# Strassen's seven products for the down projection of a hybrid decoder layer

## The chip, the cores and the metric

The kernel runs on one core of a Trainium2 chip. The metric is device time in microseconds (us) for one execution of the whole layer; a smaller time is better. The engines are named as in the profile: PE (TensorE, with PEld for its weight loads), DVE (VectorE), ACT (ScalarE), POOL (GpSimd) and SP (SyncE, which here only issues transfers).

## What is computed

The layer takes x (512 tokens by 1024 features, float32), adds the output of two mixers (an mLSTM group and a sparse-attention group), and then a gated MLP, on which the change works:

```python
h = rms_norm(x, norm_ffn[l])
u = causal_dwconv(h @ w_up[l], ffn_conv_w[l], ffn_conv_b[l])   # 1024 -> 2 * 2816, conv of width 3
gate, val = u[..., :D_FF], u[..., D_FF:]
x = x + (jax.nn.silu(gate) * val) @ w_down[l]                  # 2816 -> 1024
...
return rms_norm(x, norm_final)
```

## The kernel before

Every float32 product is made as three products of rounded parts: each operand is split into a high part (ACT copies it to the fp32r type: `whi`, `gh`) and a low part (DVE or POOL subtracts the high part from it: `wlo`, `gl`), and PE adds high·high, low·high and high·low into one PSUM bank. `split` (L121) makes the two parts.

Weights come from DRAM in pieces of 1 MB (`raw`, two buffers, issued by SP), and each piece is split in two halves of 128x1024, into four buffers of `whi` and four of `wlo`. All engines follow one order that is written out in the code, each engine its own part of it in sequence, so an instruction that waits holds up all behind it on its engine. `take` hands out the next split piece and puts splits of pieces up to two ahead into a queue, `later`; `merge` pops one entry of it after each step of PE's work.

The up projection has 44 groups (22 chunks of 128 features, a gate and a value for each). A group is 24 matmuls of 512 columns into one of three banks (tags mm, mm, av). Behind each group ACT and DVE do the convolution from the bank (`conv3`, L999); for a gate ACT also does the silu; for a value POOL multiplies gate and value (L1018), and the product is split into `gh` and `gl` (22 chunks x 512 tokens).

The down projection holds eight accumulators, 4 tiles of 128 tokens x 2 halves of 512 features, in all eight banks. It runs over 22 chunks; a chunk needs one split weight piece and makes 8 x 3 = 24 matmuls of 512 columns (L1053 to L1055). The last four chunks are done tile by tile, so that the final norm of a tile (square on ACT, mean, gain, power on POOL, scale, store) lies beside the matmuls of the next; the last 512 columns are done as two pieces of 256.

Of the kernel before, what the change touches and what calls it, by code (L numbers as in the profile page):

```python
# [44 lines left out]
def hybrid_layer(ctx: ExitStack, tc: tile.TileContext, a, out):  # L45
# [14 lines left out]
    def bank(tag):  # L60
        return ps.tile([128, 512], F32, name="bank_" + tag, tag=tag, bufs={"mm": 2, "lg": 3, "tp": 2, "av": 1}[tag])
# [5 lines left out]
        return bank(mm_tags[-1])  # L67


    raws, subs, nload, nsplit = [], [], [0], [0]  # L70

    def add_raw(pieces, cuts, place=None):

        raws.append([pieces, place])
        for view, shape in cuts:
            subs.append([len(raws) - 1, view, shape, None])

    def load_to(n):
        while nload[0] < min(n, len(raws)):
            i = nload[0]  # L80
            raw = raws[i][1]
            if raw is None:
# [21 lines left out]
    def split_next():  # L104
        i = nsplit[0]
        r, view, shape, _ = subs[i]
        load_to(r + 1)
        src = view(raws[r][1])
        cnt = shape[0] * shape[1]
        hi = wp.tile([128, 1024], F32R, name="whi", tag="whi", bufs=4)  # L110
        lo = wp.tile([128, 1024], F32R, name="wlo", tag="wlo", bufs=4)
        hv = hi[:, :cnt].rearrange("p (a b) -> p a b", a=shape[0])
        lv = lo[:, :cnt].rearrange("p (a b) -> p a b", a=shape[0])

        split(hv, lv, src, nc.gpsimd if i in on_pool else None)
        subs[i][3] = (hv, lv)
        nsplit[0] += 1
        if i + 1 < len(subs) and subs[i + 1][0] != r:
            load_to(r + 3)
# [58 lines left out]
    for c2 in range(NF // 2):  # L178
        add_raw(rows(a["w_down"], 2 * c2), [row_cut(0), row_cut(1)])
    sub_i, look = [0], [2]  # L180
    on_pool = set(range(6, 25)) | {35,37,39}

# [822 lines left out]
    ys = {}  # L1005
# [40 lines left out]
    banks = [bank(tag) for tag in ("lg", "lg", "lg", "tp", "tp", "av", "mm", "mm")]  # L1046
    gh, gl = ffn["gh"], ffn["gl"]

    def down(c, t, hf, w, b_=None, c0=0, c1=512, first=0):
        sl, cs = slice(t * 128, (t + 1) * 128), slice(c0, c1)  # L1050
        wh, wl = w
        b_ = (b_ or banks[2 * t + hf])[:, cs]
        nc.tensor.matmul(b_, gh[:, c, sl], wh[:, hf, cs], start=(c == first), stop=False)  # L1053
        nc.tensor.matmul(b_, gl[:, c, sl], wh[:, hf, cs], start=False, stop=False)  # L1054
        nc.tensor.matmul(b_, gh[:, c, sl], wl[:, hf, cs], start=False, stop=(c == NF - 1))  # L1055

    for c in range(NF - 4):
        (w,) = take()
        for t in range(NB):
            for hf in range(2):  # L1060
                down(c, t, hf, w)
            if later:
                later.popleft()()
    o_v = out.rearrange("b (t p) d -> (b t) p d", p=128)
    ws = take(4)
    for t in range(NB):
        pieces = ((0, 0, 512), (1, 0, 512)) if t < NB - 1 else ((0, 0, 512), (1, 0, 256), (1, 256, 512))
        ssf = small.tile([128, 3], F32, name="ssf")
        xn = ffn["p"].tile([128, D], F32, name="xn", tag="yc", bufs=3)
        for i, (hf, c0, c1) in enumerate(pieces):  # L1070

            own = bank("lg") if c0 else None
            for j in range(4):
                down(NF - 4 + j, t, hf, ws[j], own, c0, c1, NF - 4 if c0 else 0)
            cs = slice(hf * 512 + c0, hf * 512 + (c1 if c0 else 512))
            nc.vector.tensor_tensor(x[t][:, cs], (own or banks[2 * t + hf])[:, c0:(c1 if c0 else 512)], x[t][:, cs], OP.add)
            cs = slice(hf * 512 + c0, hf * 512 + c1)
            nc.scalar.activation(xn[:, cs], x[t][:, cs], AF.Square, accum_out=ssf[:, i:i + 1])

            ms = small.tile([128, 1], F32, name="ms", bufs=4)  # L1080
            if i == 0:
                nc.vector.tensor_scalar(ms, ssf[:, 0:1], 1.0 / D, EPS, op0=OP.mult, op1=OP.add)
            else:
                nc.vector.scalar_tensor_tensor(ms, ssf[:, i:i + 1], 1.0 / D, last, op0=OP.mult, op1=OP.add)
            last = ms
            (nc.vector if i + 1 == len(pieces) else nc.gpsimd).tensor_tensor(x[t][:, cs], x[t][:, cs], gfin[hf][:, c0:c1], OP.mult)
        r = small.tile([128, 1], F32, name="r", bufs=4)
        nc.gpsimd.tensor_tensor(r, last, mhalf[:, :1], OP.pow)
# [36 lines left out]
```

## Time and profile before

| | |
|---|---|
| time, median of 3 runs (lowest, highest) | 673.66 us (672.49, 675.17) |
| the profiled execution | 673.75 us, its span 672.0 us |
| busy share of the span: PE, DVE, ACT, POOL | 97 %, 60 %, 44 %, 23 % |
| bytes moved by transfers | 62.22 MB, 93 GB/s on average |

A page of the profile gives the busy time of each engine, and a chain of work followed back from the last instruction. Busy time of PE is modelled for each matmul with its start and length, and matmuls overlap; what counts is the distance between starts. An idle time is shown in brackets behind the instruction that ended it, with what released it.

### The profile page before, as it was taken

Reading aid. Unit: us, or ns where it says so; the run is one execution under the profiler, and the core shown is the slowest. Engines: PE = TensorE matmul, PEld = TensorE weight load, DVE = VectorE, ACT = ScalarE, POOL = GpSimd, SP = SyncE. Lnnn points to the kernel's source line nnn. Section 1 sums busy time; section 2 is a strip of 40 time slices with the busy share of each in tenths; the row PEclk is TensorE's granted clock in tenths of the full one; section 3 lists DMA queues with packets and bytes.
Section 4 is the critical chain, followed back from the end, with each engine's and each line's share of the span. In section 5 each row is a group of like instructions: output and inputs, shape, how many; then the busy total and the mean of one; then the engine's idle time right before and its main releaser. Section 6 shows DMA issues by size and latency. Waiting matters only on the chain.

```text
span 672.0 us, 8948 instructions
## 1 busy us (share of the span) xinstructions
PE 654.9 (97%) x3455; PEld 559.4 (83%) x3455; DVE 403.2 (60%) x741; ACT 296.3 (44%) x510; POOL 157.0 (23%) x162
## 2 busy tenths in 40 slices
PE   7999999989999999999999999999999999999996
PEld 5987889768889998889888888888888888888885
DVE  4688999979756765765465555555555562222234
ACT  5555255756756424453444453444444441111223
POOL 2132576223452306322101101010101110000023
PEclk9999999989999999999999999999999999999998
DMA  9321543010111221313033312331133233322102
GB/s 300 124 66 62 176 139 123 3 64 1 63 63 54 74 81 46 90 68 126 1 125 126 110 58 83 126 126 62 63 126 125 91 130 134 117 88 101 62 32 94
DMA packets 47194, 62.22 MB, mean 93 GB/s; under 512 B 3795, under 2 KB 40855, under 8 KB 47152
## 3 DMA queue, kind: packets, MB, share of 16 engines
q1 hardware_dynamic: 45488, 56.83, 25.4%
q0 software_dynamic: 944, 3.25, 1.6%
q10 hardware_dynamic: 720, 1.57, 0.7%
q8 instruction: 27, 0.44, 0.3%
q14 instruction: 15, 0.12, 0.1%
HBM read 59.53 MB, written 2.12 MB: 92 GB/s over the span
## 4 chain that ended last, share of the span: by engine, by line
PE 78%; DVE 13%; issue 3%; POOL 2%; ACT 2%; DMA 1%; POOLq 0%; DVEq 0%; ACTq 0%
PE bank_mm L192 9%; PE bank_mm L194 9%; PE bank_mm L193 9%; PE bank_av L192 4%; PE bank_av L193 4%; PE bank_av L194 4%; DVE score L513 3%; DVE m L510 3%; DVE score L495 2%; PE bank_lg L1055 2%; PE bank_lg L1053 2%; PE bank_lg L1054 2%; PE bank_mm L363 2%; PE bank_av L711 2%; PE bank_mm L236 2%
## 5 line engine op out<-in xcount | busy, mean ns | idle before, releaser
L123 DVE TENSOR_TENSOR wlo<-raw,whi 128x1024 fp32r<-128x1024 f32 x78 | 97.4, 1253 | 120.6 <-ACT whi L122 120.6
L122 ACT ACTIVATE whi<-raw 128x1024 fp32r<-128x1024 f32 x100 | 104.8, 1051 | 95.4 <-PE bank_mm L1054 73.4
L192 PE MATMUL bank_mm<-fh,whi 128*128 128x512 f32 (+1 forms) x248 | 93.2, 376 | 0.0
L194 PE MATMUL bank_mm<-fh,wlo 128*128 128x512 f32 (+1 forms) x248 | 93.2, 376 | 0.0
L193 PE MATMUL bank_mm<-fl,whi 128*128 128x512 f32 (+1 forms) x248 | 93.1, 376 | 0.0
L1018 POOL TENSOR_TENSOR yc<-yc 128x512 f32<-128x512 f32 x22 | 28.4, 1290 | 213.4 <-DVE yc L1002 213.4
L123 POOL TENSOR_TENSOR wlo<-raw,whi 128x1024 fp32r<-128x1024 f32 x22 | 54.2, 2466 | 72.0 <-ACT whi L122 52.2
L192 PEld LDWEIGHTS bank_mm<-fh,whi 128*128 128x128 f32 x248 | 46.7, 188 | 8.5
L194 PEld LDWEIGHTS bank_mm<-fh,wlo 128*128 128x128 f32 x248 | 46.7, 188 | 8.5
L193 PEld LDWEIGHTS bank_mm<-fl,whi 128*128 128x128 f32 x248 | 46.7, 188 | 8.3
L192 PE MATMUL bank_av<-fh,whi 128*128 128x512 f32 (+1 forms) x128 | 48.2, 376 | 0.0
L194 PE MATMUL bank_av<-fh,wlo 128*128 128x512 f32 (+1 forms) x128 | 48.1, 376 | 0.0
L193 PE MATMUL bank_av<-fl,whi 128*128 128x512 f32 (+1 forms) x128 | 48.1, 376 | 0.0
L122 ACT ACTIVATE gh<-yc 128x512 fp32r<-128x512 f32 x22 | 13.9, 632 | 69.8 <-POOL yc L1018 69.8
L192 PE MATMUL bank_mm<-hh,whi 128*128 128x512 f32 (+1 forms) x112 | 44.0, 393 | 0.0
L123 DVE TENSOR_TENSOR gl<-yc,gh 128x512 fp32r<-128x512 f32 x22 | 15.2, 693 | 47.7 <-ACT gh L122 47.7
L194 PE MATMUL bank_mm<-hh,wlo 128*128 128x512 f32 (+1 forms) x112 | 42.4, 379 | 0.0
L193 PE MATMUL bank_mm<-hl,whi 128*128 128x512 f32 (+1 forms) x112 | 42.2, 377 | 0.0
L236 PE MATMUL bank_mm<-whi,hh 128*128 128x256 f32 x112 | 32.6, 291 | 0.0
L1011 ACT ACTIVATE yc<-yc 128x512 f32<-128x512 f32 x22 | 13.9, 632 | 42.3 <-DVE yc L1002 42.3
L237 PE MATMUL bank_mm<-whi,hl 128*128 128x256 f32 x112 | 31.6, 282 | 0.0
L238 PE MATMUL bank_mm<-wlo,hh 128*128 128x256 f32 x112 | 31.6, 282 | 0.0
(326 smaller groups left out, 1549.9 us busy)
## 6 DMA issues: line engine op xcount, KB each, us to landing
raw<-in_w_up_dram SPq DMA_DIRECT2D x22, 1024.0 KB, 5.1
raw<-in_w_in_dram SPq DMA_DIRECT2D x13, 1024.0 KB, 5.0
raw<-in_w_down_dram SPq DMA_DIRECT2D x11, 1024.0 KB, 4.8
raw<-in_w_out_dram SPq DMA_DIRECT2D x4, 1024.0 KB
T<-skew POOLq DMA_DIRECT2D x1, 2048.0 KB, 8.6
x<-in_x_dram SPq DMA_DIRECT2D x3, 512.0 KB, 5.2
out_dram<-xn SPq DMA_DIRECT2D x4, 256.0 KB, 2.1
out_dram<-xn ACTq DMA_DIRECT2D x4, 256.0 KB, 2.5
```

The lines of the kernel that those rows point to most:

```text
L122: nc.scalar.activation(hv, src, AF.Copy)
L123: (eng or nc.vector).tensor_tensor(lv, src, hv.bitcast(F32), OP.subtract)
L192: nc.tensor.matmul(ps_, lh, rh, start=first, stop=False)
L193: nc.tensor.matmul(ps_, lh, rl, start=False, stop=False)
L194: nc.tensor.matmul(ps_, ll, rh, start=False, stop=last)
L236: nc.tensor.matmul(st["ps"], ah, wh[:, i, :], start=(k == 0), stop=False)
L237: nc.tensor.matmul(st["ps"], al, wh[:, i, :], start=False, stop=False)
L238: nc.tensor.matmul(st["ps"], ah, wl[:, i, :], start=False, stop=(k == 7))
L510: nc.vector.max(m8[0], acc)
L513: nc.vector.match_replace(acc, m8[0], acc, TAKEN)
L1011: nc.scalar.activation(ys[c][:, 0, :], ys[c][:, 0, :], AF.Silu)
L1018: nc.gpsimd.tensor_tensor(y[:, 0, :], y[:, 0, :], y[:, 1, :], OP.mult)
```

## The change

The output y·W (y: 512 tokens x 2816, W: 2816 x 1024) is cut in halves in all three directions: y into A11, A12 (tokens 0 to 255; chunks 0 to 10 and 11 to 21) and A21, A22 (tokens 256 to 511), W into B11, B12, B21, B22. Where the kernel before makes eight products of halves, the new one makes seven of sums of quarters. In the order of the code they are A11·B11, A12·B21, S2·T2, S1·T1, S3·T3, S4·B22 and A22·T4, with S1 = A21+A22, S2 = S1-A11, S3 = A11-A21, S4 = A12-S2 and T1 = B12-B11, T2 = B22-T1, T3 = B22-B12, T4 = B21-T2. Below they are products 0 to 6. A product has 11 chunks x 2 token tiles x 3 = 66 matmuls of 512 columns; its weights come in six pieces, five of 128x1024 (two chunks, 12 matmuls) and one of 128x512 (6 matmuls). The results are added to x from four pairs of banks.

The weight sums T1 to T4 are made in the up projection, in 11 rounds, one for each pair of weight rows: POOL issues a load of 1 MB into a buffer `prep`, DVE makes four subtractions of 128x512, POOL issues a store of 1 MB into a DRAM tensor `tq`. A round has 12 steps, spread evenly over the up projection. S1 and S3 are made by DVE in the second half of the up projection, S2 and S4 in products 0 and 2. The operand of product i+1 is split during product i.

```diff
+    cut2 = [(k, min(2, HF - k)) for k in range(0, HF, 2)]
+    tq = [dram.tile([128, 4, n, 512], F32, name=f"tq{j}") for j, (k, n) in enumerate(cut2)]
...
+    def half_place(i):
+        def f():
+            if i % 4 in (0, 2) and i < 4:
+                halfbufs.append(wp.tile([128, 2048], F32, name="raw", tag="raw", bufs=2))
+            return halfbufs[i % 4 // 2][:, i % 2 * 1024:(i % 2 + 1) * 1024]
+        return f
...
+            y, g = ys.pop(c), ffn["y"]
             conv3(y[:, 1, :], pz, NF + c)
-            nc.gpsimd.tensor_tensor(y[:, 0, :], y[:, 0, :], y[:, 1, :], OP.mult)
+            nc.gpsimd.tensor_tensor(g[:, c, :], y[:, 0, :], y[:, 1, :], OP.mult)
             def parts():
-                split(ffn["gh"][:, c, :], ffn["gl"][:, c, :], y[:, 0, :])
+                if c < HF:
+                    split(ffn["a"][0][:, c, :], ffn["a"][1][:, c, :], g[:, c, :256])
+                else:
+                    nc.vector.tensor_tensor(ffn["s1"][:, c - HF, :], g[:, c - HF, 256:], g[:, c, 256:], OP.add)
...
+            def third():
+                d = c - HF
+                nc.vector.tensor_tensor(g[:, d, 256:], g[:, d, :256], g[:, d, 256:], OP.subtract)
...
+        return [load, rest, rest, rest, lambda: comb(0, 1, 0), lambda: comb(1, 3, 1), lambda: comb(3, 3, 0),
+                lambda: comb(2, 2, 3), rest, store, rest, rest]
...
-    merged(main)
+    merged(main, (0.0, 0.99, [f for k in range(HF) for f in prep_steps(k)]))
...
+    run = ((0, 0, True, operand(1, a12) + [lambda z=z: second(z) for z in thirds]),
+           (1, 1, True, operand(2, s2) + add(0, 0, 0)),
+           (2, 2, True, operand(3, s1) + add(1, 0, 0) + [lambda z=z: fourth(z) for z in thirds]),
+           (3, 3, True, operand(4, s3) + add(2, 0, 1) + add(0, 0, 1)),
+           (4, 2, False, operand(5, s2) + add(3, 1, 1) + add(0, 1, 1)),
+           (5, 3, False, operand(6, a22) + add(2, 1, 1) + add(0, 1, 0)))
+    for i, b, fresh, sides in run:
+        merge(product(i, b, fresh, cut2), (0.0, 0.95, sides), later=later)
+    ends = add(3, 0, 1) + [lambda: final(0, 0, 512), lambda: final(0, 512, 1024), lambda: store(0),
+                           lambda: final(1, 0, 512), lambda: final(1, 512, 1024), lambda: store(1),
+                           lambda: final(2, 512, 1024), lambda: final(3, 512, 1024)]
+    merge(product(6, 2, False, cut2[:4]), (0.0, 1.0, ends), later=later)
...
+    ws = [(k + j, [w_[:, j, :] for w_ in w]) for (k, n), w in zip(cut2[4:], take(2)) for j in range(n)]
+    own = bank("lg")
+    for c, w in ws:
+        mm_down(6, c, 0, w, pair[2][0], last=c == HF - 1)
+    final(2, 0, 512, (pair[2][0], 0, 512))
+    store(2)
```

**The border between up and down projection, on DVE.** Before, the last convolution (L1001, L1002) is followed by the split of the last product and then by weight splits alone:

```order
L1001 SCALAR_TENSOR_TENSOR yc<-bank_av,fw,yc 128x510
L1002 SCALAR_TENSOR_TENSOR yc<-bank_av,fw,yc 128x511
L123 TENSOR_TENSOR gl<-yc,gh 128x512
```

Now the last S1 and S3 stand there (L1047, which waits for POOL's last multiplication, and L1052), then the low part of the third weight piece of product 0, and the splits of the operand of product 1 (`bl`), which lie in the place of the normed input:

```order
L1024 SCALAR_TENSOR_TENSOR yc<-bank_av,fw,yc 128x510
L1025 SCALAR_TENSOR_TENSOR yc<-bank_av,fw,yc 128x511
L1047 TENSOR_TENSOR s_3320<-y 128x256
L1052 TENSOR_TENSOR y<-y 128x256
L125 TENSOR_TENSOR wlo<-raw,whi 128x1024
L125 TENSOR_TENSOR bl<-y,bh 128x1024 x2
L125 TENSOR_TENSOR wlo<-raw,whi 128x1024
L125 TENSOR_TENSOR bl<-y,bh 128x768
L125 TENSOR_TENSOR wlo<-raw,whi 128x1024
L1118 TENSOR_TENSOR s_4980<-s_3320,y 128x1024
```

The weight splits, which stood next to each other, are now every second instruction of DVE.

**The last product, on ACT.** Before, the last 20 weight splits stand ahead of all norms (`xn,ssf<-x` is the square, `xn<-x,r` the scaling by POOL's result):

```order
L122 ACTIVATE whi<-raw 128x1024 x20
L1078 ACTIVATE xn,ssf<-x_79 128x512 x2
L1091 ACTIVATE xn<-x_79,r 128x512
L1092 DMA out_dram<-xn 128x512
```

Now the norms of token tiles 0 and 1 (x_85, x_86) stand among the last splits, the fourth to the sixth weight piece of product 6:

```order
L1151 ACTIVATE xn,ssf<-x_85 128x512
L124 ACTIVATE whi<-raw 128x1024
L1151 ACTIVATE xn,ssf<-x_85 128x512
L1168 ACTIVATE xn<-x_85,r 128x512
L1169 DMA out_dram<-xn 128x512
L1151 ACTIVATE xn,ssf<-x_86 128x512
L124 ACTIVATE whi<-raw 128x1024
L1151 ACTIVATE xn,ssf<-x_86 128x512
L1168 ACTIVATE xn<-x_86,r 128x512
L1169 DMA out_dram<-xn 128x512
L124 ACTIVATE whi<-raw 128x512
L1151 ACTIVATE xn,ssf<-x_87 128x512
```

The splits of the last two weight pieces have moved behind the scaling and the store of tile 0, and the very last behind those of tile 1 too.

**A round of weight sums, on POOL.** Before, POOL has only its multiplications in the up projection (`L1018`, 22 in a row). Now a load and a store stand between them:

```order
L1087 DMA tq_80<-prep 512x1x512
L1041 TENSOR_TENSOR y<-yc 128x512
L1079 DMA prep<-in_w_down_dram 128x2x1024
L1041 TENSOR_TENSOR y<-yc 128x512
L1087 DMA tq_81<-prep 512x1x512
```

A load waits for the landing of the store ahead of it, since there is one `prep` buffer, and a store waits for DVE's fourth subtraction.

## Rows read from the trace of the kernel before

**Rows 1.** The page: the span, and the chain that ended last, by engine.

```profile
span 672.0 us, 8948 instructions
...
PE 78%; DVE 13%; issue 3%; POOL 2%; ACT 2%; DMA 1%; POOLq 0%; DVEq 0%; ACTq 0%
```

**Rows 2.** Busy time by stage: PE, PEld, DVE, ACT, POOL; clock, DMA share, GB/s.

```profile
321.00:545.30 224.30, 224.30 (x996) 186.03 (x996) 125.04 (x146) 98.39 (x127) 27.08 (x21) 1.00 0.28 94
545.30:665.20 119.90, 119.90 (x541) 99.67 (x539) 36.46 (x45) 29.54 (x39) 9.77 (x10) 1.00 0.28 97
```

**Rows 3.** Timeline: first down matmul; one weight split of the down stage.

```profile
545.33 0.39 PE L1053 MATMUL bank_lg<-whi,gh 128*128 128x512 f32 x1
...
616.02 1.06 ACT L122 ACTIVATE whi<-raw 128x1024 fp32r<-128x1024 f32 x1 [4.38 <-PE bank_mm L1054]
```

**Rows 4.** Groups by form, down stage: count, busy us, mean ns, idle before.

```profile
L123 DVE TENSOR_TENSOR wlo<-raw,whi 128x1024 fp32r<-128x1024 f32 x21 | 25.6, 1225 | 72.2 <-ACT whi L122 72.2
L122 ACT ACTIVATE whi<-raw 128x1024 fp32r<-128x1024 f32 x20 | 21.0, 1058 | 73.4 <-PE bank_mm L1054 73.4
```

**Rows 5.** Timeline at the border, ACT, DVE and POOL.

```profile
545.53 0.78 ACT L1000 ACTIVATE yc<-bank_av,fw 128x512 f32<-128x512 f32 x1 [1.07 <-PE bank_av L194]
...
547.13 0.75 DVE L1002 SCALAR_TENSOR_TENSOR yc<-bank_av,fw,yc 128x511 f32<-128x511 f32 x1
...
548.05 1.29 POOL L1018 TENSOR_TENSOR yc<-yc 128x512 f32<-128x512 f32 x1 [9.59 <-DVE yc L1002]
...
549.91 2.94 ACT L122 ACTIVATE whi<-raw 128x1024 fp32r<-128x1024 f32 x3
```

**Rows 6.** Groups by form, up stage: POOL's multiplication, DVE's split of its result.

```profile
L1018 POOL TENSOR_TENSOR yc<-yc 128x512 f32<-128x512 f32 x22 | 28.4, 1290 | 213.4 <-DVE yc L1002 213.4
...
L123 DVE TENSOR_TENSOR gl<-yc,gh 128x512 fp32r<-128x512 f32 x22 | 15.2, 693 | 47.7 <-ACT gh L122 47.7
```

**Rows 7.** Transfers: issuing queue, count, KB each, median us to landing.

```profile
raw<-in_w_up_dram SPq DMA_DIRECT2D x22, 1024.0 KB, 5.1
...
T<-skew POOLq DMA_DIRECT2D x1, 2048.0 KB, 8.6
x<-in_x_dram SPq DMA_DIRECT2D x3, 512.0 KB, 5.2
```

**Rows 8.** Timeline: POOL splits beside a quiet and a busy DVE.

```profile
278.88 2.40 POOL L123 TENSOR_TENSOR wlo<-raw,whi 128x1024 fp32r<-128x1024 f32 x1 [4.31 <-ACT whi L122]
...
300.46 6.17 POOL L123 TENSOR_TENSOR wlo<-raw,whi 128x1024 fp32r<-128x1024 f32 x2 [0.89 <-ACT whi L122]
...
302.13 2.23 DVE L123 TENSOR_TENSOR wlo<-raw,whi 128x1024 fp32r<-128x1024 f32 x1
```

**Rows 9.** Timeline of the end: norms of token tiles 2 and 3.

```profile
659.80 0.69 DVE L1076 TENSOR_TENSOR x<-bank_av,x 128x512 f32<-128x512 f32 x1 [0.71 <-PE bank_av L1055]
...
660.52 0.63 ACT L1078 ACTIVATE xn<-x 128x512 f32<-128x512 f32 x1 [1.62 <-DVE x L1076]
...
661.06 0.19 ACT L1078 ACTIVATION_READ_ACCUMULATOR xn<-x 128x1 f32 x1
...
661.52 0.93 POOL L1088 TENSOR_TENSOR r<-ms,mhalf 128x1 f32<-128x1 f32 x1 [1.24 <-DVE ms L1084]
...
662.48 0.73 ACT L1091 ACTIVATE xn<-x,r 128x512 f32<-128x512 f32 x1 [1.24 <-POOL r L1088]
...
662.89 0.68 DVE L1076 TENSOR_TENSOR x<-bank_mm,x 128x512 f32<-128x512 f32 x1
...
664.53 0.68 DVE L1076 TENSOR_TENSOR x<-bank_mm,x 128x512 f32<-128x512 f32 x1
...
665.07 0.28 PE L1055 MATMUL bank_lg<-wlo,gh 128*128 128x256 f32 x1
...
666.94 0.42 DVE L1086 TENSOR_TENSOR x<-x,gain 128x256 f32<-128x256 f32 x1
...
668.55 0.34 ACTq L1092 DMA_DIRECT2D out_dram<-xn  x1
```

More of the change, by code (lines that the diff above doesn't have):

```diff
@@ L81, in load_to @@
             raw = raws[i][1]
-            if raw is None:
+            if callable(raw):
+                raws[i][1] = raw = raw()
+            elif raw is None:
                 raws[i][1] = raw = wp.tile([128, 2048], F32, name="raw", tag="raw", bufs=2)
@@ L118, in split_next @@
         if i + 1 < len(subs) and subs[i + 1][0] != r:
-            load_to(r + 3)
+            load_to(r + (5 if i + 1 >= first_down[0] else 3))
     def split(hv, lv, src, eng=None):
@@ L1057, in hybrid_layer @@
[L1057 to L1063, printed above, removed]
-    o_v = out.rearrange("b (t p) d -> (b t) p d", p=128)
[L1065 to L1086, printed above, removed]
@@ new lines, in hybrid_layer, with operand @@
+    pair = [[bank(tag) for tag in tags] for tags in (("lg", "lg"), ("lg", "tp"), ("tp", "av"), ("mm", "mm"))]
+    y, s1 = ffn["y"], ffn["s1"]
+    s2 = ffn["p"].tile([128, HF, 256], F32, name="s2", tag="s2", bufs=1)
+    ops = [ffn["a"], [big.tile([128, HF, 256], F32R, name=n, tag=t) for n, t in (("bh", "B0"), ("bl", "B1"))]]
+    thirds = [slice(0, 4), slice(4, 8), slice(8, HF)]
+    def operand(i, src):
+        return [lambda z=z: split(ops[i % 2][0][:, z, :], ops[i % 2][1][:, z, :], src[:, z, :]) for z in thirds]
@@ new lines, in add, with f, second, fourth @@
+    def add(b, t2, d2):
+        def f(t):
+            xs = x[2 * t2 + t][:, d2 * 512:(d2 + 1) * 512]
+            nc.vector.tensor_tensor(xs, pair[b][t], xs, OP.add)
+        return [lambda t=t: f(t) for t in range(2)]
+    def second(z):
+        nc.vector.tensor_tensor(s2[:, z, :], s1[:, z, :], y[:, z, :256], OP.subtract)
+    def fourth(z):
+        nc.vector.tensor_tensor(s2[:, z, :], y[:, HF + z.start:HF + z.stop, :256], s2[:, z, :], OP.subtract)
+    def mm_down(i, c, t, w, b_, c0=0, c1=512, first=False, last=False):
+        (gh, gl), (wh, wl) = ops[i % 2], w
+        sl, cs = slice(t * 128, (t + 1) * 128), slice(c0, c1)
+        nc.tensor.matmul(b_[:, cs], gh[:, c, sl], wh[:, cs], start=first, stop=False, skip_group_check=True)
+        nc.tensor.matmul(b_[:, cs], gl[:, c, sl], wh[:, cs], start=False, stop=False, skip_group_check=True)
+        nc.tensor.matmul(b_[:, cs], gh[:, c, sl], wl[:, cs], start=False, stop=last, skip_group_check=True)
@@ new lines, in product, with part, final @@
+    def product(i, b, fresh, chunks):
+        st = {}
+        def part(k, n, j, t):
+            if j == 0 and t == 0:
+                (st["w"],) = take()
+            mm_down(i, k + j, t, [w_[:, j, :] for w_ in st["w"]], pair[b][t], first=fresh and k + j == 0, last=k + j == HF - 1)
+        return [lambda k=k, n=n, j=j, t=t: part(k, n, j, t) for k, n in chunks for j in range(n) for t in range(2)]
+    o_v = out.rearrange("b (t p) d -> (b t) p d", p=128)
+    fin = {}
+    def final(t, c0, c1, sums=None):
+        if sums:
+            b_, e0, e1 = sums
+            nc.vector.tensor_tensor(x[t][:, e0:e1], b_, x[t][:, e0:e1], OP.add)
+        if t not in fin:
+            fin[t] = [ffn["p"].tile([128, D], F32, name="xn", tag="yc", bufs=3), small.tile([128, 3], F32, name="ssf"), 0, None]
+        xn, ssf, i, sofar = fin[t]
+        nc.scalar.activation(xn[:, c0:c1], x[t][:, c0:c1], AF.Square, accum_out=ssf[:, i:i + 1])
+        ms = small.tile([128, 1], F32, name="ms", bufs=4)
+        if i == 0:
+            nc.vector.tensor_scalar(ms, ssf[:, 0:1], 1.0 / D, EPS, op0=OP.mult, op1=OP.add)
+        else:
+            nc.vector.scalar_tensor_tensor(ms, ssf[:, i:i + 1], 1.0 / D, sofar, op0=OP.mult, op1=OP.add)
+        fin[t][2:] = [i + 1, ms]
+        (nc.vector if sums else nc.gpsimd).tensor_tensor(x[t][:, c0:c1], x[t][:, c0:c1],
+                                                         gfin[c0 // 512][:, c0 % 512:c0 % 512 + c1 - c0], OP.mult)
@@ L1087, in hybrid_layer, with store @@
+    def store(t):
+        xn, _, _, ms = fin[t]
         r = small.tile([128, 1], F32, name="r", bufs=4)
-        nc.gpsimd.tensor_tensor(r, last, mhalf[:, :1], OP.pow)
+        nc.gpsimd.tensor_tensor(r, ms, mhalf[:, :1], OP.pow)
         nc.vector.tensor_scalar(xn[:, :512], x[t][:, :512], r, None, op0=OP.mult)
@@ L1092, in hybrid_layer @@
         nc.scalar.dma_start(o_v[t][:, 512:], xn[:, 512:])
+    a12, a22, s3 = y[:, HF:, :256], y[:, HF:, 256:], y[:, :HF, 256:]
+    run = ((0, 0, True, operand(1, a12) + [lambda z=z: second(z) for z in thirds]),
[10 more added lines that the diff above has]
+    merge(product(6, 2, False, cut2[:4]), (0.0, 1.0, ends), later=later)
+    while later:
+        later.popleft()()
+    ws = [(k + j, [w_[:, j, :] for w_ in w]) for (k, n), w in zip(cut2[4:], take(2)) for j in range(n)]
[4 more added lines that the diff above has]
+    store(2)
+    for c, w in ws:
+        mm_down(6, c, 1, w, pair[2][1], 0, 256, last=c == HF - 1)
+    final(3, 0, 256, (pair[2][1], 0, 512))
+    for c, w in ws:
+        mm_down(6, c, 1, w, own, 256, 512, first=c == ws[0][0], last=c == HF - 1)
+    final(3, 256, 512, (own[:, 256:], 256, 512))
+    store(3)
 def bucket_onehot():
```

42 lines of the change are left out of this document (28 added, 14 removed).

## The prediction

> **What bounds the kernel now.** I first read the chain that ended last: 78 % of the span is PE [rows 1]. Then the two stages of the MLP: PE is busy in all of the up projection and all of the down projection, at a granted clock of 1.00, while DVE is busy for 125 of 224 us in the one and 36 of 120 us in the other [rows 2]. So in the down projection only the number of matmuls counts. Its pace: a weight split repeats every 4.38 + 1.06 = 5.44 us [rows 3], a chunk is 24 matmuls, so one takes 5.44 / 24 = 0.2267 us from start to start. The wait in that row is the other thing to see: ACT has run ahead until all four split buffers are full, and is let on by PE's end of an older chunk. Weight preparation is never late; DVE waits 72 us of the stage behind ACT [rows 4].
>
> The profiled execution took 673.75 us, 0.09 us over the median of 673.66, so the sum made against it stands for both. In it the down projection begins at 545.33 [rows 3]; its last matmul starts at 665.07 and ends, 0.12 us a piece in this tail of 256 columns, at 665.19 [rows 9]. From there to the end of the span are 6.81 us.
>
> **What the change removes.** 528 half products become 7 x 66 = 462 matmuls of 512 columns, of the same shape with the same weight loads. 66 x 0.2267 = 14.96 us go from a stage in which nothing but PE ends last. If all the rest hides, the profiled time becomes 658.8 us.
>
> **What it adds beside the up projection.** DVE: 11 rounds of four subtractions of 128x512 at 0.69 [rows 6], 30 us; 22 sums and differences of 128x256 at 0.42 (the form of rows 9), 9 us; the old split of 22 x 0.69 = 15 shrinks to 11 x 0.42 = 5. So 125 + 29 = 154 of 224 us. The cover is PE's own 224 us, and a slack behind it: a bank comes free about 3 us after its group and is wanted again two groups (10.9 us) later. What may break the cover is the wait inside a round. The store is released by the fourth subtraction, the next load by the store's landing, the next subtraction by the load's landing; behind that subtraction on DVE stand the convolutions that free PE's banks, and behind the load on POOL the gate multiplications. A round has 12 steps of 1.29 steps of PE's work, 12 x 1.29 x 1.36 = 21 us. From the order, a store leaves some 3 us after a convolution, the load goes behind the next multiplication but one convolution later, at about 9 us or when the store has landed, and the first subtraction stands at 18.6 us; the convolution behind it is due at 21.8. Store and load may take 18.6 - 3.1 = 15.5 us together before DVE is held. No row has a 1 MB transfer from POOL. SP's takes 5.1 us, POOL's of 2 MB 8.6 us [rows 7]; so one takes between 5.1 and 8.6, two between 10.2 and 17.2. The nearest row in size is SP's, and beside the weight loads some wait is likely; I take 6.5 each, 13 us, which hides. I cost the up projection at 0, with 0 to 14 us as its bounds (17.2 - 15.5 = 1.7 us in each of up to 8 rounds after the slack is gone).
>
> **What it adds beside the down projection.** For a product DVE has five low parts of 1.23 and one of 0.69 (6.8 us), the operand's two of 1.23 and one of 0.96 (a 128x768, halfway between the rows; 3.4 us), and adds of 0.69. Product 2 has most, 6.8 + 3.4 + 2 x 0.69 + 3.4 for S4 = 15.0 us; product 0 has 13.7, product 1 11.6, products 3 to 5 13.0. PE needs 66 x 0.2267 = 14.96 us a product. So DVE is 88 % busy and still behind nothing, since four split buffers let it run two to three pieces ahead. ACT has 9 us a product. A half piece of 512 KB takes 5.2 us at most [rows 7] and four places give it 10.9. So the middle of the stage is PE's pace. Not so its two ends, which I went through instruction by instruction in the order of the code.
>
> **The beginning.** Let U be 545.33. ACT evacuates the last group at U + 0.2, DVE convolves until U + 2.55, POOL multiplies from U + 2.7 to U + 4.0 [rows 5]. Until then DVE is held at the last S1. S1 and S3 take 0.42 each, to 4.85; the low part of the third weight piece ends at 6.1. PE wants it at 5.44 + 2 x 0.2267 = 5.9: 0.2 us late. Two splits of the operand follow (to 8.55), then the low part of the fourth piece, to 9.8; PE wants it at 8.16 + 0.45 + 0.2 = 8.8: 1.0 us late. The fifth ends at 12.0 and is wanted at 12.5; from there DVE gains. That is 1.2 us; successive splits overlap a little (three in 2.94 us where one is 1.06 [rows 4, 5]), so I take **1.1 us**, between 0.3 and 1.5. Before, pieces last 5.44 us instead of 2.72, and the same wait was covered.
>
> **The end.** Let V be PE's end of product 5. DVE's adds to tiles 0 and 1 wait for V, then the norms come in ACT's order: square of tile 0 (0.63 + 0.19) until V + 2.4, POOL's power done at 5.5, scaling and issue of the store (0.73 + 0.34) until 6.6, a square, and only then the split of the fifth piece, 8.45; another square, 9.25; POOL's two multiplications and power for tile 1 until 11.45, scaling and issue until 12.5, and the last piece's high part at 13.15, its low part at 13.9. PE wants that piece after 54 matmuls, at 12.24. So tile 2's last product ends at 14.15 instead of 12.92. DVE is held by two squares until 14.95, adds tile 2, and is at tile 3 one chain later: 662.89 - 659.80 = 3.09 us [rows 9], 18.04. From the like add of before to the end are 672.0 - 664.53 = 7.47 us [rows 9], and one multiplication of 0.42 more stands in DVE's way now: V + 25.9. Had PE run through (48 + 9 matmuls at 0.2267, 18 of 256 columns at 0.12: 15.1 us) and the old 6.81 us followed, it were V + 21.9. So 4.0 us more.
>
> Here two engines also collide. Beside a quiet DVE POOL's split of 128x1024 takes 2.40 us; beside a busy one two took 6.17, and DVE's took 2.23 instead of 1.23 [rows 4, 8]. In product 6 POOL's four multiplications of 1.29 meet DVE's low parts. If each holds the other for its rest, the same pass gives the last high part at V + 14.9, tile 2's end at 15.8 and the end at V + 27.6: 5.7 us. The Trainium skill (SBUF — State Buffer, section "SBUF: two separate sides") says that a DVE operation with two SBUF inputs and a reading GpSimd operation shut each other out for a whole instruction; by that rule it is the 5.7, and the rows above agree. Not every pair will meet, so I take **4.9 us**, between 2.2 (only the longer chain behind PE) and 5.7.
>
> **Sum.** 673.75 - 14.96 + 1.1 + 4.9 = 664.8 us, for the median too. Its own range, from the bounds of both ends: 661.3 to 666.
>
> **The rivals.** *The ends hide*: ACT and DVE are further ahead than my pass has them, and only a part of the tail remains, 658.8 + 0.3 + 1.5 = 660.6. For it speaks that DVE idles now; against it that the waits at both ends are on POOL and PE, not on its speed. *The round of weight sums is longer than its slot*, the case on the other side: if two transfers take over 15.5 us, DVE is late by the rest in each round, and when the slack is gone PE waits for banks in the up projection. At 17.2 us it is 14 us, 664.8 + 14 = 679; it decides against the change from about 9 us on, that is at 16.6 us. For it: these transfers share the 16 DMA engines with weight loads (0.28 of their time now, about twice that then [rows 2]). Against it: 6.5 us each is well under the bound. *DVE becomes the bound in the middle*: at 88 % its 80 us in products 0 to 5 would have to grow by 12 % to reach PE's 90; with collisions and waits at 20 % it costs 6 us, 671. Against it: POOL has nothing to do there until product 6, so nobody collides. That the products are not made is no rival: the order shows 462.
>
> **How the numbers follow.** My forecast 0.58, the ends hide 0.13, long rounds 0.16 (half of it with a few us), DVE as bound 0.11, else 0.02. The time is that of the first. The range takes the first two whole, and the near halves of the other two: 660 to 671 us, with 0.15 left out above and some 0.04 below. Half a per cent is 3.4 us, about what a measurement here can tell from no change: faster is under 670.3, slower over 677. Faster: 0.58 + 0.13, and half each of the last two, 0.83; same 0.10; slower 0.07.
>
> **What would show it.** In the trace after: down projection's matmuls 0.2267 apart; the up projection as long as before (224.3 us between the same groups), with POOL's loads and stores of 1 MB landing in under 7.5 us; two gaps of PE within 10 us of the border, waiting for DVE's low parts; a gap of 1 to 3 us before the last nine matmuls of tile 2, waiting for ACT's high part behind a scaled store; from PE's last matmul to the end 8.5 to 9.7 us instead of 6.8. I am wrong if PE waits for banks in the up projection, if it waits between products 1 and 5, or if the granted clock falls in one of these gaps and doubles what follows.

## The result, and the profile after

The change makes the kernel faster: 663.82 us (median of 4 runs, 662.14 to 664.08) against 673.76 us, ratio 0.9847 with a 95 % interval of 0.9821 to 0.9872. Predicted were 664.8 us, range 660 to 671. Of the six executions of run 9 below one took 714.45 us, at a mean granted clock of 0.849, and is left out of that run's numbers.

The page of the changed kernel: its span, the busy time of the engines, the chain that ended last (its line by engine), and three rows of the transfers (issuing queue, count, KB each, median us to landing).

```profile
span 662.3 us, 9108 instructions
...
PE 640.9 (97%) x3386; PEld 546.3 (82%) x3386; DVE 479.4 (72%) x851; ACT 317.7 (48%) x537; POOL 178.3 (27%) x185
...
PE 80%; DVE 10%; issue 3%; ACT 3%; POOL 2%; DMA 1%; ACTq 0%; POOLq 0%; DVEq 0%
...
raw<-in_w_up_dram SPq DMA_DIRECT2D x22, 1024.0 KB, 6.7
...
prep<-in_w_down_dram POOLq DMA_DIRECT2D x11, 1024.0 KB, 5.4
tq<-prep POOLq DMA_DIRECT2D x11, 1024.0 KB, 4.6
```

PE still ends last [rows 1]. The weight loads take longer than before, 6.7 against 5.1 us [rows 7]; from 321 to 545.3 us ACT waits for them four times, 12.4 us in all, and PE waits for nothing. The new transfers take 5.4 and 4.6 us, 10.0 together, by their medians.

The windows by stage (us; busy time of PE, PEld, DVE, ACT, POOL; granted clock, DMA share, GB/s): the up projection in the window of before, products 0 to 5, and product 6 with the end.

```profile
321.00:545.30 224.30, 224.30 (x997) 185.96 (x996) 148.57 (x200) 88.06 (x117) 44.29 (x42) 1.00 0.57 195
545.40:636.20 90.80, 90.37 (x397) 74.17 (x396) 76.60 (x82) 52.48 (x57) 2.38 (x3) 1.00 0.62 199
636.20:662.30 26.10, 15.78 (x76) 12.64 (x74) 13.98 (x25) 10.63 (x25) 12.81 (x10) 0.86 0.23 86
```

The up projection holds as many matmuls as in [rows 2], to within one, though the DMA share doubled from 0.28 and DVE does 24 us more. A round's chain has little room. From the issue of a store to the next round's first subtraction DVE's order leaves 10.5 to 13.3 us, read round by round. Twice, where store and load took 12.7 and 12.5 us together, DVE stood still for the load's landing, for 1.92 and 2.03 us; this is the second time (POOL's store, then DVE's subtraction):

```profile
499.54 0.74 POOL L1087 DMA_DIRECT2D tq<-prep  x1 [2.95 <-DVE prep L1084]
...
512.04 0.69 DVE L1084 TENSOR_TENSOR prep<-prep 128x512 f32<-128x512 f32 x1 [2.03 <-DMA prep<-in_w_down_dram]
```

Neither reached PE, which waited for nothing in the stage.

The down projection begins at U = 545.43 (545.33 before, [rows 3]). Products 1 to 5 are without a gap: each begins 14.96 us after the one before, 66 x 0.2267.

The border, by the timeline of POOL and DVE:

```profile
548.13 1.28 POOL L1041 TENSOR_TENSOR y<-yc 128x512 f32<-128x512 f32 x1 [8.42 <-DVE yc L1025]
...
549.45 0.42 DVE L1047 TENSOR_TENSOR s<-y 128x256 f32<-128x256 f32 x1 [1.47 <-POOL y L1041]
549.91 0.43 DVE L1052 TENSOR_TENSOR y<-y 128x256 f32<-128x256 f32 x1
550.25 1.22 DVE L125 TENSOR_TENSOR wlo<-raw,whi 128x1024 fp32r<-128x1024 f32 x1
551.38 2.35 DVE L125 TENSOR_TENSOR bl<-y,bh 128x1024 fp32r<-128x1024 f32 x2
553.66 1.22 DVE L125 TENSOR_TENSOR wlo<-raw,whi 128x1024 fp32r<-128x1024 f32 x1
```

This is the chain of the prediction: DVE held until POOL's last multiplication, two sums, a low part that ends at U + 6.0, two splits of the operand, the next low part at U + 9.5. PE's steps from start to start are longer than 0.2267 by 0.2 and 0.1 from 551.09 on and by 0.55 and 0.1 from 554.15 on, 1.0 us in all with the small ones. So V, PE's end of product 5 (read as the start of the next matmul), is 636.21, and V - U is 90.78, of which 6 x 14.96 = 89.8 are matmuls.

The end, by the timeline of POOL, DVE, ACT and PE in product 6:

```profile
635.79 0.61 ACT L1151 ACTIVATE xn<-x 128x512 f32<-128x512 f32 x1
...
636.57 4.37 POOL L1159 TENSOR_TENSOR x<-x,gain 128x512 f32<-128x512 f32 x2 [86.06 <-ACT xn L1151]
...
638.13 1.66 DVE L125 TENSOR_TENSOR wlo<-raw,whi 128x1024 fp32r<-128x1024 f32 x1
639.72 1.24 DVE L1157 SCALAR_TENSOR_TENSOR ms<-ssf,ms 128x1 f32<-128x1 f32 x1
641.03 0.57 POOL L1165 TENSOR_TENSOR r<-ms,mhalf 128x1 f32<-128x1 f32 x1
641.64 0.72 ACT L1168 ACTIVATE xn<-x,r 128x512 f32<-128x512 f32 x1 [3.58 <-POOL r L1165]
...
647.79 0.72 ACT L1168 ACTIVATE xn<-x,r 128x512 f32<-128x512 f32 x1 [2.72 <-POOL r L1165]
...
648.22 0.39 PE L1128 MATMUL bank_tp<-wlo,gh 128*128 128x512 f32 x1
648.54 0.34 ACTq L1169 DMA_DIRECT2D out_dram<-xn  x1
648.98 0.63 ACT L124 ACTIVATE whi<-raw 128x512 fp32r<-128x512 f32 x1 [0.47 <-ACT xn L1168]
649.66 0.50 PE L1126 MATMUL bank_tp<-whi,gh 128*128 128x512 f32 x1 [1.06 <-ACT whi L124]
...
650.94 0.68 DVE L1147 TENSOR_TENSOR x<-bank_tp,x 128x512 f32<-128x512 f32 x1
...
652.76 0.28 PE L1128 MATMUL bank_lg<-wlo,gh 128*128 128x256 f32 x1
...
654.30 0.68 DVE L1147 TENSOR_TENSOR x<-bank_av,x 128x512 f32<-128x512 f32 x1
...
658.67 0.34 ACTq L1169 DMA_DIRECT2D out_dram<-xn  x1
```

The reader is to follow it from below: PE's step at 648.22 is 1.44 us instead of 0.23, because the last weight piece's high part stands on ACT behind a scaled store, which waits for POOL's power, which stands behind POOL's multiplications. Those are long: two in 4.37 us where two at 1.29 would be 2.6. DVE's operations beside them are long too: 1.66 for a split of 1.22, and 1.24 for a one-column operation that takes 0.16 elsewhere; this one ends with POOL's multiplication, at 640.96 and 640.94. PE's last matmul ends at 652.88, 16.7 us after V where 15.1 were the matmuls' own; from there to the end of the span are 9.4 us (6.81 before). V to the end is 26.1 us, 4.2 more than the 21.9 without cost. The sum by measured terms: 673.75 - 14.96 + 1.0 + 4.2 + 0.1 (U) = 664.09; the profiled execution took 664.08.

### The profile page after: what moved, and what is told of

Its sections match the earlier page's. It is cut to its first block, busy times and chain, and to the rows that moved or that the text cites. A ratio compares the mean times of both kernels' runs of the same rounds, so it can differ in the third digit from the quotient of the medians.

```text
span 662.3 us, 9108 instructions
## 1 busy us (share of the span) xinstructions
PE 640.9 (97%) x3386; PEld 546.3 (82%) x3386; DVE 479.4 (72%) x851; ACT 317.7 (48%) x537; POOL 178.3 (27%) x185
## 4 chain that ended last, share of the span: by engine, by line
PE 80%; DVE 10%; issue 3%; ACT 3%; POOL 2%; DMA 1%; ACTq 0%; POOLq 0%; DVEq 0%
PE bank_mm L215 10%; PE bank_mm L217 10%; PE bank_mm L216 10%; PE bank_av L217 5%; PE bank_av L216 5%; PE bank_av L215 5%; DVE score L518 2%; PE bank_mm L386 2%; PE bank_mm L259 2%; PE bank_av L734 2%; PE bank_mm L969 2%; PE bank_mm L971 2%; PE bank_mm L970 2%; PE bank_mm L260 2%; PE bank_mm L261 2%
## 5 line engine op out<-in xcount | busy, mean ns | idle before, releaser
L125 DVE TENSOR_TENSOR wlo<-raw,whi 128x1024 fp32r<-128x1024 f32 x98 | 118.7, 1214 | 55.3 <-ACT whi L124 55.3
L124 ACT ACTIVATE whi<-raw 128x1024 fp32r<-128x1024 f32 x120 | 123.1, 1028 | 72.9 <-PE bank_mm L1127 13.9
L1041 POOL TENSOR_TENSOR y<-yc 128x512 f32<-128x512 f32 x22 | 30.7, 1395 | 141.5 <-DVE yc L1025 141.5
L1159 POOL TENSOR_TENSOR x<-x,gain 128x512 f32<-128x512 f32 x6 | 10.2, 1708 | 90.9 <-ACT xn L1151 90.9
L1084 DVE TENSOR_TENSOR prep<-prep 128x512 f32<-128x512 f32 x44 | 30.1, 685 | 4.2 <-DMA prep<-in_w_down_dram 4.0
```

Of the source, the lines that this page charges most:

```text
L1041: nc.gpsimd.tensor_tensor(g[:, c, :], y[:, 0, :], y[:, 1, :], OP.mult)
L1084: nc.vector.tensor_tensor(prep[:, o, :], prep[:, x_, :], prep[:, y_, :], OP.subtract)
```

## Experiments

U, V and the pace are read from PE's timeline in every run. U itself lies between 544.4 and 548.0 (run 2 apart): 545.43 in the changed kernel, 546.50 in run 5, which changes nothing before the last chunk. It is settled ahead of the up projection: from that projection's first matmul to U are 242.1 to 242.2 us in every run but run 2. A part of the difference can be seen in the windows 120 to 160 us of two kernels (the changed kernel again, then the one with 128 bytes more padding; columns as above):

```profile
120.00:140.00 20.00, 16.61 (x96) 13.57 (x96) 18.66 (x58) 13.54 (x46) 6.21 (x10) 0.95 0.12 36
140.00:160.00 20.00, 19.61 (x120) 16.43 (x119) 16.16 (x45) 11.14 (x29) 4.01 (x5) 0.96 0.06 19
```

```profile
120.00:140.00 20.00, 16.66 (x101) 13.53 (x99) 18.61 (x59) 14.14 (x45) 7.39 (x10) 0.97 0.05 12
140.00:160.00 20.00, 20.00 (x110) 17.05 (x110) 15.10 (x44) 9.31 (x26) 3.99 (x5) 0.86 0.12 42
```

PE is idle for 3.3 to 3.4 us of the first stretch in both; in the second the granted clock (1.00 is the full 2.4 GHz) is 0.96 in one and 0.86 in the other. So single runs are compared from U to the end of the span, 116.9 us in the changed kernel, and not by their time.

**1. Without the rounds.** The weight sums are not made; products that need T1 to T4 read plain quarters of w_down instead, in the same pieces.

```diff
-            src = (tq[j][:, q] if q is not None else
-                   wd[f2 * HF + k:f2 * HF + k + n, :, d2 * 512:(d2 + 1) * 512].rearrange("k p c -> p k c"))
+            f2, d2 = (q // 2, q % 2) if q is not None else (f2, d2)
+            src = wd[f2 * HF + k:f2 * HF + k + n, :, d2 * 512:(d2 + 1) * 512].rearrange("k p c -> p k c")
...
-    merged(main, (0.0, 0.99, [f for k in range(HF) for f in prep_steps(k)]))
+    merged(main)
```

> The rounds of weight sums are left out: no loads into prep, no subtractions, no stores, and the products that use T1 to T4 read plain quarters of w_down in their place (so the output is not the layer's). My theory: the rounds are hidden wholly behind PE in the up projection, so the first down matmul starts at 545.4 us of the span as in the changed kernel, within 0.3, and the time stays within 1 us of 663.8. The rival, that the rounds and their 22 MB of traffic cost something there: the border moves forward by what they cost, and the time falls with it by 1 us or more.

Measured: 664.11 us, U 545.38, V - U 90.82, V to the end 26.2. The up projection in the same window:

```profile
321.00:545.30 224.30, 224.30 (x997) 185.96 (x996) 124.06 (x156) 90.09 (x117) 27.05 (x21) 1.00 0.30 97
```

DVE does 24 us less, half of the bytes move, and PE does the same 997 matmuls. The rounds cost nothing here.

**2. The rounds in 60 % of their time.** The same steps, spread over the first 60 % of the up projection.

```diff
-    merged(main, (0.0, 0.99, [f for k in range(HF) for f in prep_steps(k)]))
+    merged(main, (0.0, 0.6, [f for k in range(HF) for f in prep_steps(k)]))
```

> The 11 rounds are spread over the first 60 % of the up projection instead of 99 %, a slot of 12.8 us for each instead of 21. My theory: a round is a loop of load (5.4 us to landing), four subtractions with what stands between them on DVE (6 us), and store (4.6 us), some 16 to 17 us, so each is 3 to 4 us too long for the slot, DVE is held behind the first subtraction, and after about two rounds PE waits for banks: the border moves back by 9 x 3.5 - 6 = 20 to 35 us, and the time is 684 to 699. The rival, that the waits of POOL and DVE are harmless because both are ahead of PE anyway: the border stays within 2 us of 545.4.

Measured: 701.8 us, the down projection begins at 583.15. The windows of its up projection, and its waits from 321 to 582.5 us (engine, operand, line, releaser: us in total, times, longest):

```profile
321.00:480.00 159.00, 140.10 (x571) 108.87 (x570) 91.33 (x122) 49.73 (x70) 29.64 (x31) 0.96 0.55 191
480.00:545.00 65.00, 60.39 (x258) 49.10 (x257) 37.32 (x50) 23.65 (x29) 9.25 (x8) 0.95 0.39 133
545.00:583.00 38.00, 38.00 (x170) 31.46 (x169) 21.86 (x28) 14.63 (x18) 3.86 (x3) 1.00 0.38 125
```

```profile
POOL prep L1079 <- DMA tq<-prep: 39.5, 10, 5.8
DVE prep L1084 <- DMA prep<-in_w_down_dram: 31.0, 10, 6.1
...
PE bank_mm L217 <- DVE wlo L125: 9.5, 8, 3.3
PE bank_av L217 <- DVE wlo L125: 7.2, 6, 2.8
```

The rival that the place of the rounds is harmless falls: DVE and POOL, in their order, wait for each landing, and the up projection ends 37.7 us later; PE is idle for 18.9 + 4.6 us in the first two windows. The same rounds cost nothing in 99 % of the stage. Three things were not as expected. The 37.7 us and the time lie above the 20 to 35 and the 684 to 699 us that were given. PE waited mostly for low parts of the weights (9.5 + 7.2 us) rather than for banks. And the granted clock fell to 0.95 and 0.96 in the stretches with these waits, where it is 1.00 in the changed kernel. The other 14.2 of the 37.7 us are time in which PE counts as busy for longer over the same matmuls (238.5 us for 999, against 224.3 for 997); by an estimate from these windows some 10 of them are the clock's (0.04 x 159 + 0.05 x 65).

**3. The gain multiplications on DVE.** POOL keeps only the powers of product 6.

```diff
-        (nc.vector if sums else nc.gpsimd).tensor_tensor(x[t][:, c0:c1], x[t][:, c0:c1],
+        nc.vector.tensor_tensor(x[t][:, c0:c1], x[t][:, c0:c1],
```

> The six multiplications by the final gain that POOL makes go to DVE; nothing else changes place. If POOL and DVE shutting each other out is what makes the end late: the powers of tiles 0 and 1 come 0.7 and 2 us earlier, the last weight piece is split before PE wants it, PE's wait of 1.2 us ahead of tile 2's last matmuls goes below 0.3, and from PE's end of product 5 to the end of the span are 24 to 24.8 us instead of 26.1. If it is ACT's order alone (splits behind the scaled stores): DVE has 4 us more to do, the wait stays at 1 us or more and the end within 0.5 us of 26.1.

Measured: 662.49 us, U to the end 115.8, V to the end 25.0, just above the 24 to 24.8 expected and well under the rival's 25.6. PE's wait ahead of tile 2's last matmuls is gone (0.1 us stays). The same operations on DVE and ACT now:

```profile
639.45 0.15 DVE L1157 SCALAR_TENSOR_TENSOR ms<-ssf,ms 128x1 f32<-128x1 f32 x1
...
640.67 0.72 ACT L1168 ACTIVATE xn<-x,r 128x512 f32<-128x512 f32 x1 [3.03 <-POOL r L1165]
...
645.86 0.72 ACT L1168 ACTIVATE xn<-x,r 128x512 f32<-128x512 f32 x1 [1.76 <-POOL r L1165]
```

The one-column operation is back at 0.15, and the second scaled store leaves 10.1 us after V instead of 11.6. PE's end comes 1.5 us sooner after V, and the tail behind it is 0.4 us longer, with DVE's extra work. This takes away both the collisions and POOL's slower multiplications (1.29 against 0.68), so it does not part these two.

**4. More work for DVE in products 3 to 5.** Four subtractions of 128x1024 are added to each, whose result nobody reads.

```diff
+    junk = ffn["p"].tile([128, 4, 256], F32, name="junk", tag="yc", bufs=3)
+    more = [lambda: nc.vector.tensor_tensor(junk, s1[:, :4, :], y[:, :4, :256], OP.subtract)] * 4
     for i, b, fresh, sides in run:
+        sides = sides + more if i >= 3 else sides
```

> Products 3, 4 and 5 each get four more DVE subtractions of 128x1024 into a tile that nobody reads, 4 x 1.14 to 1.23 = 4.6 to 4.9 us a product beside the 12.1 us measured there. My theory: DVE has 2 to 3 us of room in each product and a lead of some 5 us through the four split buffers; three products ask for 17 us where PE takes 15, so the lead takes 2 us from each, and the time rises by 0 to 3 us. The rival that DVE is already the bound of the middle: each added operation shows in full, 14 us.

Measured: 668.94 us, V - U 90.78, V to the end 30.0. DVE's window over products 3 to 5, and PE's waits from U on:

```profile
593.00:637.00 44.00, 43.83 (x47) 1.00 0.57 178
```

```profile
PE bank_tp L1126 <- ACT whi L124: 2.4, 1, 2.4
PE bank_tp L1128 <- DVE wlo L125: 1.9, 2, 1.3
PE bank_lg L1128 <- DVE wlo L125: 0.4, 1, 0.4
```

DVE is busy for 43.83 of 44.00 us, and those products are not 0.01 us longer: the split weights ahead of PE cover it. All of the cost, 3.8 us, falls into product 6, where that lead is used up and the norms begin. The expectation had the cost at 0 to 3 us, so it was too low; the rival, that DVE bounds the middle and each us of its work is a us of time, would have been 14, in the products themselves.

**5. S1 and S3 of the last chunk later.** They go behind the operand's splits in product 0, so DVE is not held at the border.

```diff
+    held = []
...
-            later.append(parts)
+            (held if c == NF - 1 else later).append(parts)
...
-                later.append(third)
+                (held if c == NF - 1 else later).append(third)
...
-    run = ((0, 0, True, operand(1, a12) + [lambda z=z: second(z) for z in thirds]),
+    run = ((0, 0, True, operand(1, a12) + held + [lambda z=z: second(z) for z in thirds]),
```

> S1 and S3 of the last chunk, which wait for POOL's last multiplication, move on DVE from ahead of the third weight piece's low part to behind the splits of product 1's operand. My theory: DVE no longer stands still at the border, the low parts of the third and fourth piece are there when PE wants them, the gaps of PE within 10 us of the border (0.43, 0.34, 0.78 and 0.33 us between starts where 0.23 is the pace, 1.0 us in all) go, and the span is 1.0 us shorter. The rival, that these gaps come from the weight transfers at the border or from the switch itself: they stay, and the span is the same within 0.2 us measured from the border to the end.

Measured: U to the end 116.1 us, 0.8 less; V - U 89.97, with 0.2 us of gaps left; V to the end 26.1 as before. The time is 664.33 us, since U was 1.1 us later. So the order of these two sums was 0.8 of the beginning's 1.0 us; the cause of the rest is open.

**6. Norms earlier.** The first halves of the norms of tiles 0 and 1 move into product 3, and both second squares go ahead of both stores; POOL keeps its multiplications. `ms` needs eight buffers for it, which lie ahead of `gh` and `gl`.

```diff
-        ms = small.tile([128, 1], F32, name="ms", bufs=4)
+        ms = small.tile([128, 1], F32, name="ms", bufs=8)
...
-           (3, 3, True, operand(4, s3) + add(2, 0, 1) + add(0, 0, 1)),
+           (3, 3, True, operand(4, s3) + add(2, 0, 1) + add(0, 0, 1) +
+            [lambda: final(0, 0, 512), lambda: final(1, 0, 512)]),
...
-    ends = add(3, 0, 1) + [lambda: final(0, 0, 512), lambda: final(0, 512, 1024), lambda: store(0),
-                           lambda: final(1, 0, 512), lambda: final(1, 512, 1024), lambda: store(1),
+    ends = add(3, 0, 1) + [lambda: final(0, 512, 1024), lambda: final(1, 512, 1024), lambda: store(0), lambda: store(1),
```

> The order alone is changed at the end, POOL keeps its multiplications: the squares and gains of the first 512 columns of tiles 0 and 1, complete since product 2, are made in product 3, and those of the second 512 columns of both tiles stand ahead of both scaled stores. If the order on ACT makes the end late: the power of tile 0 comes about 2 us earlier, the last weight piece is split before PE's turn (no wait of 1.2 us), and from PE's end of product 5 to the end of the span are 24 to 25 us instead of 26.1. If only the collisions of POOL and DVE do: two of the four multiplications still collide there, and half of the loss stays, 25.3 us or more with a wait of PE left.

Measured: 664.64 us, V to the end 24.6 us, and PE no longer waits in product 6. So either remedy alone, POOL's part (3) or the order (6), removes the wait. But U to the end is only 0.6 us shorter, 116.4: V - U rose by 1.0 to 91.79, without a wait that the changed kernel does not have. Products 0, 2, 4 and 6 ran at 0.2325 us a matmul (0 apart from its gaps), products 1, 3 and 5 at 0.227.

**7. Both ends.** The edits of 3, 5 and 6 together, and the store of tile 2 behind the first part of tile 3's norm:

```diff
     final(2, 0, 512, (pair[2][0], 0, 512))
-    store(2)
...
     final(3, 0, 256, (pair[2][1], 0, 512))
+    store(2)
```

> The two orders of before (sums later, norms early), the gains on DVE, and tile 2's scaling moved behind tile 3's first addition and square. If both ends are made by order and collisions as the theory has it, their terms add: 1.0 us at the border, 2.0 us for PE's wait and the late norms, 1 to 2 us for the shorter chain behind PE's last matmul; from the border to the end of the span 113 us instead of 116.9, and a time of 659 to 660.5 against 663.8. The rival, that a remainder is fixed because DVE has more to do with the gains: 661.5 or more.

Measured: 663.48 us (663.12 to 664.66) against 674.74, ratio 0.9845 (0.9831 to 0.9858), no better than the change. U to the end is 115.0 us, V to the end 24.0 as hoped, and the even products are slow again. The theory of the ends held, and its gain was eaten by something that it did not know. Two explanations stood: the work moved beside these products, or the place of `gh` and `gl`, which the even products read and which the four new buffers of `ms` had moved by 128 bytes (of each partition) in the built program.

**8 to 12. The place alone.** Run 8 is the changed kernel itself, 9 is run 7 with `gh` and `gl` back at their place, 10 is the changed kernel with its tiles moved by 128 bytes; 11 and 12 move those of run 9 by 256 and by 64 bytes. The whole edit is the size of an unused tile (run 10 here; from 88 to 56 in run 9, to 120 in run 11, to 72 in run 12). The size counts elements of 4 bytes, so what the expectations of runs 9 and 10 call 32 bytes of padding are 32 elements, 128 bytes.

```diff
-    small.tile([128, 88], F32, name="pad", bufs=1)
+    small.tile([128, 120], F32, name="pad", bufs=1)
```

> The changed kernel itself, beside the two others on one chip: about 663.8 us (662.1 to 665.0), a matmul every 0.2267 us in all seven products, 90.8 us from the first to the last matmul of product 5, 116.9 us from the start of the down projection to the end of the span. It says by how much the span moves from run to run for reasons that lie ahead of the down projection.

> Both ends shortened as in the version with both ends, but 32 bytes of padding taken away, so that the operand tiles gh and gl of the even products lie at the address that they have in the changed kernel. Theory (the place of the stationary operand made the even products slower there): a matmul every 0.2267 us in all products again, 89.8 to 90.2 us from the first matmul to the end of product 5, 113.5 to 114.2 us from the start of the down projection to the end (115.0 with the other place, 116.9 in the changed kernel), and 2.5 to 3.4 us less time than the changed kernel on the same chip. Rival (the extra work beside those products made them slower): the even products stay at 0.232 us, and the stretch at 115.0 us.

> The changed kernel with 32 more bytes of padding and nothing else, so that gh and gl lie 128 bytes further on. Theory (place): the even products go to about 0.2325 us a matmul while the odd ones keep 0.2267, so that products 0 to 5 take 1.0 to 1.5 us more (91.8 to 92.3 us), and the stretch to the end 118 to 118.7 us against 116.9. Rival (the extra work in those products): nothing moves, 90.8 and 116.9 us.

> The version with both ends at the old place, with 64 more elements of padding a partition, so that everything behind the padding, gh and gl among it, lies 256 bytes further on. If the pace repeats every 256 bytes: 0.2267 us a matmul in all products, 89.8 to 90.2 us over products 0 to 5, 113.5 to 114.2 us from the start of the down projection to the end (113.7 without the step). If only the old place itself is good: the even products at 0.2325, 91.0 us, and 115 us.

> The same with 16 more elements of padding, so that gh and gl lie 64 bytes further on, as far again as half of the step that made the even products slower. If the pace goes by the distance from the place in steps of 256 bytes, the even products run between 0.2267 and 0.2325; if there are only two paces, at one of these. The odd products keep 0.2267. The stretch to the end lies between 113.5 and 115.2 us.

Measured (us; product 2 and product 3 from their first matmul to the first of the next one; U to V and U to the end of the span; runs 8, 9 and 10 on one chip, 11 and 12 on one):

| run | moved by | product 2 | product 3 | U to V | U to end | time |
|---|---|---|---|---|---|---|
| 8, the changed kernel | 0 | 14.96 | 14.96 | 90.8 | 116.9 | 663.86 (663.72 to 664.87) |
| 10, only moved | 128 B | 15.35 | 14.98 | 91.7 | 117.9 | 667.61, one run |
| 7, both ends | 128 B | 15.35 | 14.98 | 91.0 | 115.0 | 663.48 |
| 9, both ends, old place | 0 | 14.96 | 14.96 | 90.0 | 113.7 | 660.55 (660.51 to 661.80) |
| 11, both ends | 256 B | 14.96 | 14.96 | 90.0 | 113.7 | 660.61, one run |
| 12, both ends | 64 B | 15.40 | 14.99 | 91.2 | 115.2 | 661.38, one run |

Groups by form from 545 us on, of run 10 and then of run 11 (line, tiles, shape, count, busy us, mean ns of one):

```profile
L1126 PE MATMUL bank_mm<-whi,bh 128*128 128x512 f32 x44 | 17.1, 389 | 0.0
...
L1126 PE MATMUL bank_av<-whi,gh 128*128 128x512 f32 x30 | 11.8, 395 | 0.0
L1128 PE MATMUL bank_av<-wlo,gh 128*128 128x512 f32 x30 | 11.8, 394 | 0.0
L1127 PE MATMUL bank_av<-whi,gl 128*128 128x512 f32 x30 | 11.8, 394 | 0.0
```

```profile
L1127 PE MATMUL bank_av<-whi,gh 128*128 128x512 f32 x30 | 11.7, 389 | 0.0
L1128 PE MATMUL bank_av<-whi,gl 128*128 128x512 f32 x30 | 11.7, 389 | 0.0
L1129 PE MATMUL bank_av<-wlo,gh 128*128 128x512 f32 x30 | 11.7, 389 | 0.0
```

The rival falls: run 10 does the work of run 8 in the same order, and its even products are slower by 0.39 us each, while the products that read `bh` and `bl` (kept in a pool that is opened ahead of the padding's) change by 0.02 at most. A step of 256 bytes gives the old pace, 64 and 128 give a slower one. Run 12 bears out neither half of its expectation: at 64 bytes the pace is not between the two known ones but slower than both. Run 10's stretch grew by 0.9 us, where 1.1 to 1.8 was expected: in product 6 the slower pace hides in PE's wait, since V to the end is 26.1 as in run 8. Its time rose by more, with a later U (548.0), as shown at the head of this section.

Run 9 is faster than both kernels: 660.55 against 673.61 us of the kernel before, ratio 0.9807 (0.9794 to 0.9819), and 3.3 us under the changed kernel on the same chip. It has the same work on DVE as run 7, so run 7's rival, that a remainder stays because DVE has more to do with the gains, falls too.

## Why the prediction was right

- **What is removed**, 14.96 us: the pace after is 0.2267, and products 1 to 5 take 14.96 us each.
- **The up projection at 0**: right, shown by run 1 and by the equal count of matmuls. But two sizes in its sum were wrong, and that they made up for each other was luck: the transfers take 10.0 us together where 13 were given, and the bound at which DVE is held is 10.5 to 13.3 us where 15.5 were given. By the trace's bounds transfers of 13 us would have held DVE in five of ten rounds; as it was, two rounds held it, for some 2 us each, and PE did not wait. The slack of the banks that the prediction names would explain this, but no run measures it. What comes of it when each round holds DVE run 2 shows, with a slot cut to 0.6 of its length; at which length the cost begins is open. The prediction had PE wait for banks in that case; run 2 shows it waiting first for low parts of the weights, which are in the same DVE queue behind the subtraction.
- **The middle at 0**: right, and with more room than "88 % busy and still behind nothing" says. Run 4 had DVE at 99.6 % in products 3 to 5 without a delay there. What such load costs appears in product 6.
- **The beginning**, 1.1 us predicted, 1.0 measured, with both gaps at the pieces named. Run 5 takes 0.8 of it away by the order of two sums.
- **The end**, 4.9 us predicted, 4.2 measured. The mechanism was as told: a high part behind a scaled store on ACT, and 9.4 us from PE's end where 8.5 to 9.7 were given. The trace follows the pass without collisions (V + 25.9) almost step by step: the last high part ends at V + 13.4 (13.15 given), DVE's adds of tiles 2 and 3 begin at V + 14.7 and 18.1 (14.95 and 18.04), the span ends at V + 26.1. So of the 0.9 us put on top for collisions 0.2 show. This does not mean that collisions are cheap: POOL's first two multiplications took 1.8 us longer, and run 3, without them and with the gains on the faster engine, ends at V + 25.0. The pass has the square of tile 0 end at V + 2.4; in the trace its first half, of columns that are complete since product 2, begins before V, and POOL's first multiplication begins at V + 0.4. By these times the earlier start made up for the collisions; no run parts the two, and that they came out even is luck. The rule that the prediction took from the Trainium skill (SBUF — State Buffer, section "SBUF: two separate sides"), that such a pair shuts out one another for a whole instruction, fits the rows where they met (4.37, 1.66 and 1.24 us). The 5.7 us that the prediction worked out by it did not come; not every pair met, and the prediction said so.
- The forecast that "the ends hide" falls: both were visible, 5.2 us together.

Errors of -0.1 at the beginning and -0.7 at the end, with U 0.1 later, make the difference of 0.7 us between 664.8 and 664.1; the median, 663.82, is 1.0 us under the forecast. No term was wrong in sign.

## What to carry to other kernels

When a matmul stage that PE bounds is shortened, work through its two ends instruction by instruction: here the middle hid the added work, and both costs stood at the ends. Of what both ends cost, 3.2 of 5.2 us came back through order and the choice of engine, with no work left out. When an edit adds or resizes a tile, look at the pace of the untouched matmuls first: in run 6 a shift of the operands took back 1.0 of the 1.6 us that the edit had gained.

## What was not expected of the hardware

- The pace of the same matmuls depends on where `gh` and `gl` begin: 0.2267 us at one place and 256 bytes behind it, 0.2325 at 128 bytes, 0.2334 at 64 bytes (15.11 and 15.17 us over 65 steps). The clock was granted at 1.00 throughout. Which of the two tiles matters, and by what mechanism, was not tried; all tiles behind the padding moved together.
- A one-column DVE operation took 1.24 us beside POOL's multiplications, and 0.15 to 0.16 without them.
- Two executions whose kernels differ in the padding alone (runs 8 and 10) had a granted clock of 0.96 and 0.86 from 140 to 160 us, and began the down projection 2.9 us apart. Not all of this was traced to that stretch: 60 to 120 us also held 308 matmuls instead of 313. The padding moves the tiles of the attention stage too, so a share of the place in it is not excluded; but U differs by 1.5 us among kernels with these tiles at the same place (545.0 in run 3, 546.5 in run 5).
